# A quarter of the weights' low parts subtracted on GpSimd, and the builder's durations taken from a trace

## The chip, the cores and the metric

The kernel runs on one core of a Trainium2 chip. A core has TensorE (PE; its weight loads are shown as PEld), VectorE (DVE), ScalarE (ACT), GpSimd (POOL) and SyncE (SP), which here issues the loads. The metric is the device time of one execution in microseconds (us). Before the change it is 883.34 us, the median of 3 runs (882.36 to 884.08).

## The reference, cut to what matters

The reference runs four layers over 256 tokens of width 1024, in float32: two attention layers (a sliding window with sinks, then a causal one, phases `a` and `b`), and two layers that each have a mixer of dilated attention and a Mamba-2 scan (`m0`, `m1`) and a SwiGLU feed-forward part of width 2816 (`f0`, `f1`):

```python
def first_block(x, ...):                       # layers a, b
    ...
        q, k, v, z = split_proj(rmsnorm(h, norm_g[i]), w_in_a[j], N_KV_A)
        o = sliding_window_sink_attention(q, k, v, sinks_a[j])
        ...
        o = o.reshape(B, S, MIX_WIDTH) * jax.nn.silu(z)
        h = h + o @ w_out[i]
def second_block(...):                         # layers 0, 1
    ...
        h = h + hybrid_mixer(rmsnorm_2(h, norm_mix[layer]), w_in[layer], ...)
        h = h + swiglu(rmsnorm_2(h, norm_ffn[layer]), w_gate[layer], w_up[layer], w_down[layer])
    return rmsnorm_2(h, final_norm)
```

Most of the arithmetic is `h @ w` with weights that are read once.

## The kernel before

Each weight matrix is cut into units of 256 output columns, and a unit into k-tiles of 128x256. TensorE multiplies in fp32r. To keep float32's precision, each operand is split into a high part (rounded to fp32r) and a low part (the operand less its high part), and a k-tile takes three products: high by high, high by low, low by high. In the phases of the feed-forward part the first two are one matmul of 512 columns (mode `AB`); elsewhere they are separate matmuls of 256 columns.

SyncE loads a weight segment of up to 8 k-tiles (1 MB) into one of three raw buffers (`raw`, `RAW = 3`). `feed` (line 362) then splits two k-tiles at a time: `hi` is a copy on ScalarE, or on VectorE where that is 100 ns less booked, and `lo` is the subtraction `raw - hi` on VectorE (line 396). A raw buffer is free for the next load when both have read it. The 1048 k-tiles of weights make 524 such splits of 128x512 (a few at the start are of one k-tile, and the 16 columns of `dt` are split apart).

Everything else goes beside the weights' matmuls as chains: norms (their power -1/2 runs on GpSimd as a 128x2 tensor_tensor), rotary embedding, attention (scores on TensorE, softmax on VectorE and ScalarE, transposes, values), the convolution and scan of the mixers, gates.

The order on each engine is fixed when the program is built, by a list scheduler. It keeps one planned clock per engine (`self.clk`). `account` (line 251) books every instruction: it starts when its engine's clock and its chain allow, lasts `cost(...)` (line 223), and its result is ready for others `HOP` later. `run_plan` (line 487) emits the next k-tile's matmuls if their inputs are planned to be ready, steps every chain whose inputs are ready on TensorE's planned clock, and lets `feed` split ahead. `feed` waits while VectorE or ScalarE is planned more than `AHEAD` = 500 ns past TensorE, unless fewer than `URGENT` = 5 k-tiles are ready. Fixed pauses in planned time pace attention (`HEAD_A`, `HEAD_B`, `HEAD_0`, `HEAD_1`, `PAIR`), and `calm` (line 269) holds a chain back while VectorE or ScalarE is planned too far ahead. The planned durations thus set the order, not the waits: what waits for what is fixed by the data.

Of the kernel before, what the change touches and what calls it, by code (L numbers as in the profile page):

```python
# [11 lines left out]
F32 = mybir.dt.float32  # L12
F32R = mybir.dt.float32r
BF16 = mybir.dt.bfloat16
# [50 lines left out]
class Engine:  # L65


    def __init__(self, build, name, real):
        self.build, self.ename, self.real = build, name, real
# [43 lines left out]
class Build:  # L113
# [8 lines left out]
    RAW = 3  # L122
    PAGES = 64
    URGENT = 5
    HOP = 100.0
    AHEAD = 500.0
    HEAD_A = 1500.0
    HEAD_B = 1500.0
# [23 lines left out]
    def __init__(self, ctx, tc, io):  # L152
        self.tc = tc
        self.nc = Engines(self, tc.nc)
        self.clk = dict(PE=0.0, DVE=0.0, ACT=0.0, POOL=0.0)
        self.cur = Chain(None, 0.0)
        self.cur.start = 0.0
        self.count = 0
        self.io = io
        self.n = 0  # L160
        self.phase = "i"

        def pool(name, bufs, **kw):
            return ctx.enter_context(tc.tile_pool(name=name, bufs=bufs, **kw))

        self.cp = pool("const", 1)
        self.wraw = pool("wraw", self.RAW)
        self.fp = pool("f", self.PAGES)
        self.xp = pool("x", 4)
        self.up = pool("u", 2)  # L170
        self.hp = pool("h", 6)
        self.sp = pool("s", 8)
        psum = dict(space=bass.MemoryType.PSUM)
        self.pp = pool("psum", 8, **psum)
        self.banks = [0.0] * 8
        self.used = dict(mm=0, sc=0, tr=0, pv=0, out=0)
        self.sides = []
        self.ups = self.raws = 0
        self.planned = {}
        self.landing = 0.0  # L180
        self.live = self.wlive = self.most = 0
        self.kept = {}
        self.x = Timed(self)
        self.res = Timed(self)
        self.plan = []
        self.dma_i = self.cast_i = self.cast_k = self.cast_slot = 0
        self.seg_i = self.seg_k = self.seg_m = self.slot = 0
        self.dma_at = 1200.0
        self.queue = self.nc.sync
        self.units = {}  # L190
        self.bubbles = {}


    def name(self, s):
# [28 lines left out]
    def cost(self, eng, op, args, kw):  # L223
        out = kw.get("out", args[0] if args else None)
        aps = [x for x in list(args) + list(kw.values()) if hasattr(x, "shape")]
        n = 1
        for d in out.shape[1:]:
            n *= d
        cols = sum(1 for x in aps if x is not out and len(x.shape) == 2 and x.shape[1] == 1 and n > 1)
        psum = any("PSUM" in str(getattr(getattr(x, "tensor", x), "space", "")) for x in aps)  # L230
        if eng == "PE":
            if op == "transpose":
                return 110.0
            f32 = args[1].dtype == F32
            if args[1].dtype == BF16:
                return 69.0 if n == 128 else n / 2.4 * 1.02
            if f32 and out.shape[0] == 64:
                return 0.95 * n
            if n < 128:
                return 110.0 * (2 if f32 else 1)  # L240
            return n / 2.4 * (4 if f32 else 1) * 1.02
        if eng == "ACT":
            acc = "accum_out" in kw
            return (52.0 if psum else 93.0) + 0.833 * n + 93.0 * cols
        if eng == "POOL":
            return 650.0
        if op in ("tensor_copy", "tensor_scalar") and not psum:
            return 68.0 + 0.52 * n + 93.0 * cols
        return (130.0 if psum else 68.0) + 1.042 * n + 93.0 * (cols if op != "tensor_tensor_reduce" else 0)

    def account(self, eng, op, args, kw):
        c = self.cur
        dep = max([c.start] + [t for e, t in c.last.items() if e != eng])
        start = max(self.clk[eng], dep)
        end = start + self.cost(eng, op, args, kw)
        self.clk[eng] = end
        self.count += 1
        c.last[eng] = end + self.HOP
        c.ready = max(c.ready, end + self.HOP)


    def go(self, gen):
# [99 lines left out]
    def feed(self):  # L362

        nc = self.nc
        while self.dma_i < len(self.plan) and self.raws < self.RAW:
            self.feed_dma()
        while self.cast_i < self.dma_i and self.cast_slot < self.slot + self.LEAD:
            now = self.clk["PE"]
            urgent = self.cast_slot < self.slot + self.URGENT
            if not urgent and max(self.clk["DVE"], self.clk["ACT"]) > now + self.AHEAD:  # L370
                return
            s = self.plan[self.cast_i]
            if s["at"] > now:
                self.landing = s["at"]
                return
            k = s["k0"] + self.cast_k
            n = min(2, s["k1"] - k)
            if self.wlive >= self.WMIN and self.wlive + self.live + self.SPARE > self.PAGES:
                return
            self.wlive += 2  # L380
            raw = s["raw"][:, self.cast_k:self.cast_k + n, :]
            hi = self.fp.tile([P, n, S], F32R, tag="f", name=self.name("hi"))
            if s["mode"] == "dt":

                both = hi[:, :, 0:32]
                raw, hi, lo = raw[:, :, 0:16], both[:, :, 0:16], both[:, :, 16:32]
            else:
                lo = self.fp.tile([P, n, S], F32R, tag="f", name=self.name("lo"))
            at = s["at"]
            self.cur = Chain(None, at)  # L390
            self.cur.start = at
            if self.clk["DVE"] + self.SWAP < self.clk["ACT"]:
                nc.vector.tensor_copy(hi, raw)
            else:
                nc.scalar.activation(hi, raw, AF.Copy)
            nc.vector.tensor_sub(lo, raw, hi.bitcast(F32))
            for i in range(n):
                s["parts"][k + i] = ((both if s["mode"] == "dt" else hi)[:, i, :], lo[:, i, :], self.cur.ready)
            self.cast_k += n
            self.cast_slot += n  # L400
            if s["k0"] + self.cast_k == s["k1"]:
                self.cast_i += 1
                self.cast_k = 0
                if s["page"]:
                    self.drop()
                else:
                    self.raws -= 1
# [1317 lines left out]
```

## Time and profile before

| | |
|---|---|
| median of 3 runs | 883.34 us (882.36 to 884.08) |
| the profiled execution | 882.25 us, span 880.2 us |
| TensorE busy, mean granted clock | 865.3 us (98%), 0.997 |
| VectorE busy | 731.8 us (83%) |
| ScalarE busy | 556.8 us (63%) |
| GpSimd busy | 14.6 us (2%), 30 instructions |
| read from HBM | 140.15 MB, 160 GB/s over the span |

The span reaches from the first to the last instruction in the profile; the execution's own time holds some 2 us more. Names tell what an instruction writes and reads: `f__lo<-f__raw,f__hi` is a split's subtraction in a feed-forward phase. The prefix is the phase in which the tile was made (`a`, `ao` and so on: an `o` stands for the output projection of the phase). `__p` is a PSUM tile, the other names are SBUF tiles. All of the kernel's instructions carry the line of one helper, L78.

### The profile page before, as it was taken

What the parts mean: (1) busy time and instruction counts of PE and PEld (TensorE: products, weight loads), DVE (VectorE), ACT (ScalarE), POOL (GpSimd) and SP (SyncE); (2) the same over time, 40 slices, a digit from 0 to 9 for tenths busy, and PEclk for the clock granted to TensorE, in tenths of its full rate; (3) what the DMA queues carried; (4) which work ended last, traced back from release to release, by engine and by line L of the source; (5) the groups of instructions that cost most, each with busy time, mean ns of one, the idle gap of its engine ahead of it and who ended that gap; (6) DMA issues with size and microseconds to landing.
All of it is one profiled execution on the core that took longest, in us unless ns stands there. A gap on an engine that the chain in (4) does not pass through costs nothing.

```text
span 880.2 us, 16862 instructions
## 1 busy us (share of the span) xinstructions
PE 865.3 (98%) x6451; PEld 793.9 (90%) x6451; DVE 731.8 (83%) x1652; ACT 556.8 (63%) x1325; POOL 14.6 (2%) x30
## 2 busy tenths in 40 slices
PE   8999999999999999999999999999999999999996
PEld 7987999889999789888888889999899888889996
DVE  6999899998899998899988668889878898998431
ACT  6378763677688885666666445579655666666321
POOL 0000010000000000000000000000000000000000
PEclk9999999999999999999999999999999999999998
DMA  8512673035543046666655637420046665665401
GB/s 315 206 74 73 225 275 130 26 107 177 199 145 108 26 132 215 200 226 224 234 207 179 234 127 274 158 73 25 2 137 217 224 229 200 240 220 187 167 1 48
DMA packets 30385, 142.30 MB, mean 162 GB/s; under 512 B 5344, under 2 KB 6880, under 8 KB 18400
## 3 DMA queue, kind: packets, MB, share of 16 engines
q1 hardware_dynamic: 30016, 141.08, 46.8%
q8 instruction: 51, 0.84, 0.4%
q14 instruction: 30, 0.25, 0.1%
q10 hardware_dynamic: 288, 0.14, 0.1%
HBM read 140.15 MB, written 1.05 MB: 160 GB/s over the span
## 4 chain that ended last, share of the span: by engine, by line
PE 66%; issue 21%; DVE 6%; ACT 4%; DMA 2%; SPq 0%; POOL 0%; POOLq 0%; DVEq 0%
PE m__p L78 20%; PE f__p L78 15%; PE mo__p L78 9%; PE b__p L78 8%; PE fo__p L78 7%; PE bo__p L78 3%; PE ao__p L78 3%; PE a__p L78 1%; DVE a__lo L78 1%; DVE a__sm L78 1%; ACT m__m L78 1%; DMA cst<-cst 1%; DMA fo__raw<-wa 1%; DVE a__pe L78 1%; DVE a__rope L78 1%
## 5 line engine op out<-in xcount | busy, mean ns | idle before, releaser
L78 PE MATMUL f__p<-mo__x,f__hi 128*128 128x512 f32 x492 | 174.6, 396 | 0.0
L78 DVE TENSOR_TENSOR f__lo<-f__raw,f__hi 128x512 fp32r<-128x512 f32 x186 | 123.0, 687 | 21.7 <-ACT f__hi L78 21.1
L78 PE MATMUL f__p<-mo__x,f__lo 128*128 128x256 f32 x492 | 138.0, 280 | 0.0
L78 PEld LDWEIGHTS f__p<-mo__x,f__hi 128*128 128x128 f32 x492 | 92.3, 188 | 21.5
L78 ACT ACTIVATE f__hi<-f__raw 128x512 fp32r<-128x512 f32 x186 | 104.6, 621 | 0.0
L78 PEld LDWEIGHTS f__p<-mo__x,f__lo 128*128 128x128 f32 x492 | 93.0, 189 | 0.0
L78 PE MATMUL fo__p<-f__r,fo__hi 128*128 128x256 f32 (+1 forms) x308 | 74.1, 322 | 0.0
L78 ACT ACTIVATE f__sum<-f__p 128x256 f32<-128x256 f32 x84 | 29.8, 383 | 56.8 <-PE f__p L78 56.7
L78 PE MATMUL f__p<-f__x,f__hi 128*128 128x512 f32 x176 | 63.6, 395 | 0.0
L78 DVE TENSOR_TENSOR m__lo<-m__raw,m__hi 128x512 fp32r<-128x512 f32 x74 | 50.2, 687 | 11.8 <-ACT m__hi L78 11.1
L78 PE MATMUL fo__p<-f__r,fo__lo 128*128 128x256 f32 x208 | 58.5, 281 | 0.0
L78 PEld LDWEIGHTS fo__p<-f__r,fo__hi 128*128 128x128 f32 x308 | 51.4, 190 | 4.4
L78 PE MATMUL m__p<-bo__x,m__hi 128*128 128x256 f32 (+1 forms) x292 | 54.2, 287 | 0.5 <-ACT m__m L78 0.5
L78 PE MATMUL mo__p<-mo__r,mo__hi 128*128 128x256 f32 x288 | 52.5, 284 | 0.0
L78 PE MATMUL a__p<-fo__x,a__hi 128*128 128x256 f32 x272 | 50.8, 287 | 0.7 <-ACT a__hi L78 0.7
L78 PE MATMUL f__p<-f__x,f__lo 128*128 128x256 f32 x176 | 49.3, 280 | 0.0
L78 DVE TENSOR_TENSOR fo__lo<-fo__raw,fo__hi 128x512 fp32r<-128x512 f32 (+1 forms) x60 | 37.3, 669 | 11.9 <-ACT fo__hi L78 9.3
L78 PEld LDWEIGHTS m__p<-bo__x,m__hi 128*128 128x128 f32 (+1 forms) x292 | 44.8, 188 | 2.4 <-issue 1.3
L78 PEld LDWEIGHTS mo__p<-mo__r,mo__hi 128*128 128x128 f32 x288 | 44.8, 192 | 0.2 <-issue 0.2
L78 ACT ACTIVATE m__hi<-m__raw 128x512 fp32r<-128x512 f32 x66 | 40.0, 635 | 7.3 <-DMA m__raw<-w 7.3
L78 PEld LDWEIGHTS a__p<-fo__x,a__hi 128*128 128x128 f32 x272 | 42.1, 191 | 2.1 <-ACT a__hi L78 1.3
L78 ACT ACTIVATE fo__hi<-fo__raw 128x512 fp32r<-128x512 f32 (+2 forms) x61 | 31.7, 580 | 17.4 <-DMA fo__raw<-w 10.0
(540 smaller groups left out, 2465.0 us busy)
## 6 DMA issues: line engine op xcount, KB each, us to landing
f__raw<-wu SPq DMA_DIRECT2D x20, 1024.0 KB, 4.8
f__raw<-wg SPq DMA_DIRECT2D x19, 1024.0 KB, 4.8
m__raw<-w SPq DMA_DIRECT2D x17, 1024.0 KB, 4.8
f__raw<-wd SPq DMA_DIRECT2D x9, 1024.0 KB, 4.9
b__raw<-wb SPq DMA_DIRECT2D x7, 1024.0 KB, 6.4
fo__raw<-wd SPq DMA_DIRECT2D x7, 1024.0 KB, 4.9
mo__raw<-wo SPq DMA_DIRECT2D x12, 512.0 KB, 3.7
fo__raw<-w SPq DMA_DIRECT2D x5, 1024.0 KB, 4.9
```

The lines of the kernel that those rows point to most:

```text
L78: return fn(*args, **kw)
```

## The change

In `feed`, the subtraction goes to GpSimd or to VectorE, whichever the builder plans to finish it sooner; `t` is the time at which the high part is planned to be ready. The split of `dt` stays on VectorE. A counter notes how many went where; about a quarter go to GpSimd. The planned durations and hops are replaced by ones set to those of a trace; GpSimd's was 650 ns for every instruction and is now 950 ns under 64 elements and 100 + 2.3 ns per element above, 1278 ns for a split.

```diff
-    HOP = 100.0
+    HOP = dict(PE=210.0, DVE=140.0, ACT=150.0, POOL=200.0)
...
+        self.share = [0, 0]
...
-            f32 = args[1].dtype == F32
-            if args[1].dtype == BF16:
+            dt, rows = args[1].dtype, args[1].shape[0]
+            if dt == BF16:
                 return 69.0 if n == 128 else n / 2.4 * 1.02
-            if f32 and out.shape[0] == 64:
-                return 0.95 * n
+            if dt == F32R:
+                return max(110.0, 6.7 + 0.4427 * n)
             if n < 128:
-                return 110.0 * (2 if f32 else 1)
-            return n / 2.4 * (4 if f32 else 1) * 1.02
+                return 224.0
+            if out.shape[0] == 64:
+                return 15.0 + 1.0 * n
+            if rows == 64:
+                return 44.0 + 0.92 * n
+            return 1.69 * n
         if eng == "ACT":
-            acc = "accum_out" in kw
-            return (52.0 if psum else 93.0) + 0.833 * n + 93.0 * cols
+            acc = kw.get("accum_out") is not None
+            return (52.0 if psum else 93.0) + 0.833 * n + 93.0 * (cols - acc) + 93.0 * acc
         if eng == "POOL":
-            return 650.0
+            return 950.0 if n < 64 else 100.0 + 2.3 * n
+        if op == "reciprocal":
+            return 195.0
+        if op == "tensor_copy" and out.dtype == F32R:
+            return 68.0 + 0.754 * n
         if op in ("tensor_copy", "tensor_scalar") and not psum:
-            return 68.0 + 0.52 * n + 93.0 * cols
-        return (130.0 if psum else 68.0) + 1.042 * n + 93.0 * (cols if op != "tensor_tensor_reduce" else 0)
+            return 68.0 + 0.52 * n + 63.0 * cols
+        if op == "stream_shuffle":
+            return 100.0 + 1.042 * n
+        return 78.0 + 1.042 * n + 63.0 * (cols if op != "tensor_tensor_reduce" else 0)
...
-        c.last[eng] = end + self.HOP
-        c.ready = max(c.ready, end + self.HOP)
+        c.last[eng] = end + self.HOP[eng]
+        c.ready = max(c.ready, end + self.HOP[eng])
...
-            nc.vector.tensor_sub(lo, raw, hi.bitcast(F32))
+
+            t = max(t for t in self.cur.last.values())
+            late = [max(t, self.clk[e]) + self.cost(e, "tensor_sub", (lo, raw), {}) for e in ("DVE", "POOL")]
+            sub = nc.gpsimd if late[1] <= late[0] and s["mode"] != "dt" else nc.vector
+            sub.tensor_sub(lo, raw, hi.bitcast(F32))
+            self.share[sub is nc.gpsimd] += 1
```

## Rows read from the trace of the kernel before

**Rows 1.** The page's first part: busy us (share of the span) and instructions per engine.

```profile
PE 865.3 (98%) x6451; PEld 793.9 (90%) x6451; DVE 731.8 (83%) x1652; ACT 556.8 (63%) x1325; POOL 14.6 (2%) x30
```

**Rows 2.** Waits of TensorE: who waited for whom, us in total, times, longest.

```profile
PE a__p L78 <- ACT fo__x L78: 1.1, 1, 1.1
...
PE m__p L78 <- ACT m__m L78: 0.7, 2, 0.5
...
PE ao__p L78 <- DVE a__s L78: 0.6, 1, 0.6
PE mo__p L78 <- ACT mo__pt L78: 0.6, 1, 0.6
PE ao__p L78 <- DVE ao__r L78: 0.4, 1, 0.4
PE mo__p L78 <- ACT mo__xg L78: 0.4, 1, 0.4
```

**Rows 3.** Busy time by stretch: stretch and length, each engine's busy us (xinstructions), clock, DMA.

```profile
40.00:80.00 40.00, 39.41 (x332) 33.40 (x331) 38.99 (x139) 29.76 (x100) 0.00 (x0) 1.00 0.23 80
240.00:320.00 80.00, 78.69 (x681) 72.18 (x680) 76.23 (x192) 67.55 (x192) 0.31 (x3) 1.00 0.29 93
340.00:540.00 200.00, 200.00 (x1199) 178.18 (x1198) 166.43 (x320) 121.16 (x257) 0.69 (x1) 1.00 0.61 211
680.00:820.00 140.00, 140.00 (x837) 123.42 (x836) 123.12 (x224) 88.82 (x182) 1.07 (x1) 1.00 0.64 220
820.00:860.00 40.00, 40.00 (x337) 40.00 (x337) 15.00 (x24) 12.54 (x24) 0.00 (x0) 1.00 0.14 48
```

**Rows 4.** Groups of VectorE over the span: xcount | busy us, mean ns | idle before.

```profile
L78 DVE TENSOR_TENSOR f__lo<-f__raw,f__hi 128x512 fp32r<-128x512 f32 x186 | 123.0, 687 | 21.7 <-ACT f__hi L78 21.1
L78 DVE TENSOR_TENSOR m__lo<-m__raw,m__hi 128x512 fp32r<-128x512 f32 x74 | 50.2, 687 | 11.8 <-ACT m__hi L78 11.1
```

**Rows 5.** Groups of VectorE between 40 and 80 us.

```profile
L78 DVE TENSOR_TENSOR a__lo<-a__raw,a__hi 128x512 fp32r<-128x512 f32 x16 | 10.8, 687 | 0.1
...
L78 DVE TENSOR_TENSOR a__rope<-a__rope,a__rot 128x512 f32<-128x512 f32 x4 | 2.7, 687 | 0.0
```

**Rows 6.** Groups of VectorE between 240 and 320 us.

```profile
L78 DVE TENSOR_TENSOR m__lo<-m__raw,m__hi 128x512 fp32r<-128x512 f32 x33 | 22.7, 687 | 3.3 <-ACT m__hi L78 3.0
L78 DVE TENSOR_TENSOR m__acc<-m__acc,m__tap 128x512 f32<-128x512 f32 x14 | 9.6, 685 | 0.0
L78 DVE TENSOR_TENSOR m__m<-m__m,m__cb 128x512 f32<-128x512 f32 x12 | 8.1, 684 | 0.0
```

**Rows 7.** Four powers of GpSimd in order of time: start us, us, what.

```profile
115.90 2.79 POOL L78 TENSOR_TENSOR b__s<-b__s,mhalf 128x2 f32<-128x2 f32 x1 [91.00 <-ACT b__hi L78]
...
223.55 0.69 POOL L78 TENSOR_TENSOR m__s<-m__s,mhalf 128x2 f32<-128x2 f32 x1 [1.30 <-PE m__p L78]
...
365.33 0.69 POOL L78 TENSOR_TENSOR f__s<-f__s,mhalf 128x2 f32<-128x2 f32 x1 [30.73 <-DVE f__s L78]
...
637.09 1.06 POOL L78 TENSOR_TENSOR m__s<-m__s,mhalf 128x2 f32<-128x2 f32 x1 [36.72 <-DVE m__s L78]
```

**Rows 8.** VectorE in order of time, beside those powers.

```profile
115.64 2.49 DVE L78 TENSOR_TENSOR b__lo<-b__raw,b__hi 128x512 fp32r<-128x512 f32 x4
...
365.17 0.75 DVE L78 TENSOR_TENSOR f__sum<-f__p,f__sum 128x256 f32<-128x256 f32 x2
...
636.93 0.68 DVE L78 TENSOR_TENSOR m__lo<-m__raw,m__hi 128x512 fp32r<-128x512 f32 x1
637.53 0.69 DVE L78 TENSOR_TENSOR m__acc<-m__acc,m__tap 128x512 f32<-128x512 f32 x1
638.16 0.69 DVE L78 TENSOR_TENSOR m__lo<-m__raw,m__hi 128x512 fp32r<-128x512 f32 x1
```

**Rows 9.** Low parts' tiles (f__lo; m__lo from 310.5 us): xcount, durations, first and last start.

```profile
L78 DVE TENSOR_TENSOR f__lo<-f__raw,f__hi x186: 680/685/694, 366.4 to 804.8; 128x512 fp32r<-128x512 f32 x186
...
L78 PE MATMUL fo__p<-f__r,f__lo x112: 279/282/286, 478.2 to 828.9; 128*128 128x256 f32 x112
...
L78 PE MATMUL mo__p<-m__r,m__lo x10: 279/283/288, 310.6 to 314.2; 128*128 128x256 f32 x10
L78 DVE TENSOR_TENSOR m__lo<-m__raw,m__hi x2: 683/684/685, 311.1 to 313.0; 128x512 fp32r<-128x512 f32 x2
```

## The prediction

> **What bounds the kernel now.** I read the shares of the engines first. TensorE is busy for 865.3 of 880.2 us, VectorE for 731.8, ScalarE for 556.8, and GpSimd for 14.6 [rows 1]. TensorE bounds the kernel, if its busy time is full. A matmul's modelled end overlaps the next one, so "busy" does not prove that. I therefore compared the pace of stretches in the table of busy time by stretch: from 820 to 860 us VectorE works for only 15.0 of 40 us, nothing holds TensorE up, and it runs 337 matmuls; from 40 to 80 us, with VectorE at 38.99 of 40 us, it runs 332, some of them the dearer fp32 ones of attention [rows 3]. So even where VectorE is full, TensorE keeps nearly its free pace.
>
> Next I read TensorE's waits. They are eleven rows of 7.8 us in all, from 1.1 down to 0.4 us each. Five, of 2.7 us together, lie between the start and the tail: the softmax sums (0.6) and the split of the gated output (0.4) from VectorE, the decay factors (0.7), the transposed probabilities (0.6) and the scaled inputs of the scan (0.4) from ScalarE [rows 2]. That is about what a relieved VectorE and better planning can give back: 0.3% of the span.
>
> Last I asked where VectorE has room. Between 40 and 80 us it idles 40.00 - 38.99 = 1.0 us, between 240 and 320 us 80.00 - 76.23 = 3.8 us. In the two FFN stretches it idles 200 - 166.4 = 33.6 and 140 - 123.1 = 16.9 us [rows 3].
>
> **The change part by part.** The weights are 1048 k-tiles, and one split takes two: 524 subtractions of 128x512, each 0.687 us long on VectorE [rows 4]. Issued back to back they cost it less: four take 2.49 us, so 0.60 us follows from (2.49 - 0.69) / 3 [rows 8]. A quarter is 131, so VectorE loses 131 x 0.60 = 79 us of work. Where TensorE is full that is worth nothing. It is worth something only at the two waits that VectorE ends: -1.0 us. The three waits on ScalarE stay.
>
> The price on GpSimd is not in this trace. Its nearest rows are the power of a 128x2 tile, 0.69 us, and the longest of them, 2.79 us [rows 7]; the edit itself writes 100 + 2.3 x 512 = 1278 ns. I take 1.28 us, which lies between these rows; 131 of them are 168 us, a fifth of the span, so GpSimd has room.
>
> What they do to VectorE decides. The small power shows it. It takes 0.69 us at 223.55 us, when VectorE is idle, and 0.69 us at 365.33 us, when VectorE adds from PSUM. It takes 1.06 us at 637.09 us: VectorE had just begun a subtraction with two SBUF inputs at 636.93, which ended at 637.61, and the power ended 0.54 us behind that. It takes 2.79 us at 115.90 us, beside four such subtractions in a row, which end at 118.13 us; it ends 0.56 us later [rows 7, 8]. So GpSimd stands still while VectorE reads two tensors from SBUF. The reverse shows only faintly, since the power reads two elements: the next VectorE instruction after 637.53 starts 0.63 us later instead of 0.60 [rows 8]. A GpSimd subtraction that reads 2 x 512 elements can hold VectorE between 0 and its whole 1.28 us. Nearly all that fills VectorE in these stretches has two SBUF inputs (splits, conv taps, decay products, rotary sums [rows 4 to 6]), and the builder picks GpSimd only where VectorE's planned clock is 667 ns or more behind the ready time, so VectorE has work waiting. I take 1.0 us.
>
> By that, one move takes 0.60 us from VectorE and gives it 1.0 us of standing still: +0.4 us, over 131 moves +52 us. The FFN stretches have room for their part (50 us idle), and there the low parts lie ready for long: the last split of the second FFN's up and gate tiles starts at 804.8 us, and matmuls read such tiles until 828.9 us [rows 9]. The tight stretches have none. They hold 16 + 33 = 49 splits [rows 5, 6]. Since a VectorE backlog is what the builder looks for, I put 40% of them, 20, on GpSimd rather than a quarter: 20 x 0.4 = 8 us more VectorE time against 4.8 us idle, +3 us. The ends of the range: at no hold, -20 x 0.60 = -12 us of VectorE time, which is worth at most the 2.7 us of waits; at the full 1.28 us hold, 20 x 0.68 = 14 us against 4.8, +9 us.
>
> The Trainium skill, SBUF — State Buffer, section "Who interferes with whom", says that a VectorE instruction with two SBUF inputs contends with a GpSimd instruction that reads SBUF, and that the one that starts later blocks fully. The power's four times bear out GpSimd's half of it; no row shows a long GpSimd instruction. By the rule in full the hold is the whole instruction, and the case with +9 us is the one to come.
>
> The new durations and hops change the order in which the builder emits. They add and remove no instruction. Before, the builder took a 256-column matmul for 109 ns; it now takes 120 ns, and costs VectorE less for PSUM sources (78 instead of 130 ns ahead of the elements), so its plan sees less backlog and advances attention earlier against the weight slots. Its plan had slack against the chip, and that slack goes: a chain step planned to be just in time is late by any hold. Four attention stages (a, b, m0, m1) each end where TensorE waits for such a chain; I charge one hold of 1.0 us each, +4 us. Its bounds are -1.7 us (the other three waits go too, through longer hops) and about 4 x 2.79 = +11 us (each stage loses what the longest power lost).
>
> Queues: on GpSimd's own queue the powers of the norms and the memsets of the conv inputs now stand behind subtractions. Each can be 1.28 us later. The scale rows that wait for the powers are used by units whose matmuls have already run, and other units' matmuls cover that; I take 0, at most one 1.28 us per norm, and the last one at 873 us has no split near it. A raw buffer is freed up to 0.6 us later, so SyncE issues the next load later; three buffers and a load per eight k-tiles leave room, 0. A matmul that now waits for GpSimd holds all matmuls behind it on TensorE.
>
> Sum: the profiled execution took 882.25 us (its span of 880.2 and 2.05 around it). 882.25 - 1 + 3 + 4 = 888.3 us, +6. The median of the three runs, 883.34, is 1.1 us above that execution, so I predict 889 us.
>
> **The rivals.**
> 1. Faster: GpSimd runs beside VectorE without holding it. For it: VectorE lost only 0.03 us at 637.53 [rows 8]. Against it: the waiting power. It gives back the five mid-span waits, 2.7 us: 880.6 us. It decides once the hold is under the 0.60 us that a move saves.
> 2. No change: the holds fall into the FFN stretches and the leads there swallow them; or fewer splits move in the tight stretches than I think, since the better durations show the builder less backlog. For it: TensorE's pace hardly differs between stretches [rows 3]. 883 us.
> 3. Slower by much: GpSimd is the one that starves. VectorE runs its instructions back to back, and the low part comes late by the 2.1 us that the power lost (2.79 - 0.69) on top of 1.28 us. Around 311 to 314 us a low part has no such lead: a split starts at 313.0 and ends by 313.7, and matmuls on such tiles start until 314.2 us [rows 9]. If 8 of the 20 moves stall TensorE for 2.1 us, that is +17 us: 900 us.
>
> **How the numbers follow.** Forecast (slower, some 885 to 897): 0.38. Rival 3: 0.12. Rival 2: 0.23. Rival 1: 0.27. The two slower cases make 0.50. Less than 0.2%, 1.8 us, is what a measurement of this kernel can't tell from no change. The range runs from 879.5 (the waits gone, and a little from the order) to 905 (rival 3 with the full hold), and leaves out less than 2 in 10.
>
> **What would show it.** Right: VectorE instructions longer than 0.687 us, or starting late beside a GpSimd subtraction; VectorE's busy time growing where it was full; GpSimd's subtractions well above 1.28 us where VectorE is full; TensorE's waits on low parts and on attention's chains growing from 2.7 us to 8 or more. Wrong: GpSimd subtractions of 1.28 us beside unchanged VectorE spacing of 0.60 us, and TensorE's waits at 2.7 us or below. The sign is wrong if the attention stretches run fewer TensorE waits than now.

## The result, and the profile after

The changed kernel takes 945.98 us, the median of 4 runs (944.07 to 949.01), against 883.06 us (882.36 to 884.08) for the kernel before beside it: ratio 1.0715, 95% interval 1.0694 to 1.0737. It is 63 us slower; the prediction said 889 us, with 905 as the upper end. The profiled execution took 949.01 us, its span 946.7 us.

The page of the changed kernel, engine totals and granted clock in 40 slices (tenths of full speed):

```profile
PE 890.3 (94%) x6451; PEld 812.8 (86%) x6451; DVE 782.3 (83%) x1558; ACT 532.7 (56%) x1265; POOL 202.8 (21%) x163
...
PEclk9999989799899999989999999999999899999998
```

Against [rows 1], VectorE lost 94 instructions and gained 50.5 us of busy time. GpSimd has 133 instructions more, the moved subtractions. TensorE runs the same 6451 matmuls, yet is busy 25.0 us longer, and its other time grew from 880.2 - 865.3 = 14.9 to 946.7 - 890.3 = 56.4 us. So the 66.5 us of span are 41.5 us in which TensorE stands and 25.0 us in which it works more slowly.

The waits of TensorE in the changed kernel (who waited for whom, us in total, times, longest):

```profile
PE b__p L78 <- DVE b__rope L78: 9.7, 1, 9.7
PE f__p L78 <- DVE f__sm L78: 9.4, 2, 5.0
PE m__p L78 <- DVE m__sm L78: 4.0, 2, 3.8
PE fo__p L78 <- ACT fo__hg L78: 3.5, 1, 3.5
PE b__p L78 <- DVE b__sm L78: 3.4, 1, 3.4
...
PE m__p L78 <- POOL m__s L78: 0.4, 1, 0.4
```

Where [rows 2] had no row above 1.1 us, five are now 3.4 us and more: a rotary embedding, the sums of norms (the three rows of `sm`, which TensorE multiplies by `ones`) and, in the tail, the scaled output `hg`. They are steps of chains, all but the last on VectorE. None of the twenty rows names a low part, from either engine. GpSimd appears with one power, 0.4 us.

Busy time by stretch in the changed kernel (columns as in [rows 3]), first 40 to 860 us in parts, then the longest stall and two stretches of half clock:

```profile
40.00:360.00 320.00, 296.29 (x2417) 272.63 (x2415) 286.36 (x700) 208.53 (x545) 64.67 (x50) 0.96 0.35 122
360.00:420.00 60.00, 52.28 (x351) 48.15 (x352) 49.69 (x73) 32.83 (x65) 19.64 (x14) 0.94 0.61 211
420.00:580.00 160.00, 160.00 (x907) 138.82 (x907) 132.29 (x219) 79.82 (x179) 38.07 (x27) 1.00 0.50 172
580.00:720.00 140.00, 137.42 (x1143) 127.81 (x1141) 124.34 (x269) 92.47 (x230) 24.56 (x24) 0.99 0.37 127
720.00:760.00 40.00, 33.96 (x212) 30.64 (x211) 33.20 (x52) 25.04 (x50) 13.50 (x11) 0.91 0.66 239
760.00:860.00 100.00, 100.00 (x578) 88.15 (x578) 86.35 (x130) 45.70 (x101) 23.38 (x18) 1.00 0.45 156
...
160.00:165.00 5.00, 5.00 (x44) 5.00 (x43) 4.79 (x11) 2.44 (x3) 1.29 (x1) 1.00 0.35 129
165.00:175.00 10.00, 0.32 (x3) 0.12 (x1) 9.76 (x17) 3.95 (x8) 4.38 (x3) 0.77 0.11 39
175.00:178.00 3.00, 2.94 (x14) 2.29 (x15) 3.00 (x11) 0.88 (x1) 0.00 (x0) 0.50 0.86 311
...
402.50:409.40 6.90, 5.92 (x20) 5.19 (x21) 5.33 (x11) 1.29 (x3) 1.67 (x1) 0.51 0.72 259
...
sum 42.60, PE 40.52 PEld 37.52 DVE 29.74 ACT 11.54 POOL 8.71; mean PE 5.07 PEld 4.69 DVE 3.72 ACT 1.44 POOL 1.09
```

The bodies of the two FFN parts (420 to 580 and 760 to 860 us) run with TensorE full, at full clock, as in [rows 3], although they hold some 45 of the moved subtractions. The loss lies outside them: 23.7 us of standing in 40 to 360 us (2.8 in the same stretch before), 7.7 in 360 to 420 us, 6.0 in 720 to 760 us. From 165 to 175 us TensorE runs three matmuls while VectorE is busy 9.76 of 10 us; from 175 us the granted clock is 0.50, the lower of its two levels (1.2 GHz). The last line is the sum over all eight stretches at that level: 40.52 us of TensorE's work. Three matmuls of 256 columns take 0.64 us there and 0.36 us at full clock, so I estimate that some 18 of the 40.52 us are lost to the clock: most of the 25.0.

The order of time on VectorE, then GpSimd, in that stall (start us, us, what):

```profile
168.08 0.68 DVE L78 TENSOR_TENSOR b__rope<-b__p,b__tq 128x512 f32<-128x512 f32 x1
168.67 1.33 DVE L78 TENSOR_SCALAR t<-t,cst 128x256 f32<-128x256 f32 x1
170.04 0.43 DVE L78 TENSOR_SCALAR t<-t 128x512 f32<-128x512 f32 x1
170.38 1.76 DVE L78 TENSOR_TENSOR b__rot<-b__rot,b__tq 128x512 f32<-128x512 f32 x1
172.06 2.35 DVE L78 TENSOR_TENSOR b__lo<-b__raw,b__hi 128x512 fp32r<-128x512 f32 x2
174.33 0.68 DVE L78 TENSOR_TENSOR b__rope<-b__rope,b__rot 128x512 f32<-128x512 f32 x1
...
168.58 1.27 POOL L78 TENSOR_TENSOR b__lo<-b__raw,b__hi 128x512 fp32r<-128x512 f32 x1 [5.49 <-ACT b__hi L78]
170.14 3.11 POOL L78 TENSOR_TENSOR b__lo<-b__raw,b__hi 128x512 fp32r<-128x512 f32 x2 [0.29 <-ACT b__hi L78]
```

GpSimd begins a subtraction at 168.58 and ends it at 169.85 us. VectorE's 128x256 operation, begun at 168.67, ends at 170.00 us: 1.33 us, where the twice as large one behind it takes 0.43 and the same operation in the kernel before 0.35:

```profile
159.58 0.35 DVE L78 TENSOR_SCALAR t<-t,cst 128x256 f32<-128x256 f32 x1
```

Beside GpSimd's next two, the rotary product takes 1.76 us (0.69 in the trace before) and two subtractions 2.35 instead of 0.69 + 0.60 us [rows 8]. At 168.08, fed from PSUM, an operation takes 0.68 us. The final `b__rope`, for which TensorE waits, ends at 175.01 us. The holds make some 3 us of the 9.7 (0.98 + 1.07 + 1.06); VectorE spends the rest on this chain's own steps and on work that it had queued ahead of them, such as angles for the rotary tables of later phases.

Groups of VectorE, then GpSimd, in the changed kernel (xcount | busy us, mean ns | idle before):

```profile
L78 DVE TENSOR_TENSOR f__lo<-f__raw,f__hi 128x512 fp32r<-128x512 f32 x110 | 91.3, 861 | 3.6 <-ACT f__hi L78 1.1
L78 DVE TENSOR_TENSOR f__sum<-f__p,f__sum 128x256 f32<-128x256 f32 x84 | 31.6, 415 | 1.1 <-ACT f__sum L78 1.0
L78 DVE TENSOR_TENSOR f__sum<-f__sum,f__rowh 128x512 f32<-128x512 f32 x22 | 30.2, 1374 | 0.6
L78 DVE CAST f__hi<-f__raw 128x512 fp32r<-128x512 f32 x18 | 7.6, 422 | 0.0
...
L78 POOL TENSOR_TENSOR f__lo<-f__raw,f__hi 128x512 fp32r<-128x512 f32 x46 | 61.3, 1336 | 180.5 <-ACT f__hi L78 130.1 <-DVE f__sum L78 39.5 <-PE f__p L78 10.9
L78 POOL TENSOR_TENSOR b__lo<-b__raw,b__hi 128x512 fp32r<-128x512 f32 x15 | 22.9, 1536 | 23.6 <-ACT b__hi L78 23.6
```

Two of these groups in the kernel before:

```profile
L78 DVE TENSOR_TENSOR f__sum<-f__p,f__sum 128x256 f32<-128x256 f32 x84 | 31.5, 417 | 1.0 <-ACT f__sum L78 1.0
L78 DVE TENSOR_TENSOR f__sum<-f__sum,f__rowh 128x512 f32<-128x512 f32 x22 | 15.1, 685 | 0.0
```

VectorE's subtractions rose from 687 ns in [rows 4] to 861 ns, and a product of two SBUF tensors from 685 ns before to 1374 ns, while the addition from PSUM stayed at 415 ns (417 before), although 36 of the 84 lie beside a GpSimd subtraction. With every VectorE instruction held against the median of its like in the trace before, 117 are over 100 ns longer, by 1.02 us in the median and 1.12 at most: 109 us in all, 0.82 us for each moved subtraction. The Trainium skill, SBUF — State Buffer, section "Who interferes with whom", says that the pair of SBUF ports that VectorE shares with GpSimd is an exclusive lock, whose loser blocks fully. That agrees with 1.02 of 1.27 us, less what the held instruction came late.

### The profile page after: what moved, and what is told of

Read it like the earlier page. It is cut to its first block, busy times and chain, and to the rows that moved or that the text cites. A ratio compares the mean times of both kernels' runs of the same rounds, so it can differ in the third digit from the quotient of the medians.

```text
span 946.7 us, 17141 instructions
## 1 busy us (share of the span) xinstructions
PE 890.3 (94%) x6451; PEld 812.8 (86%) x6451; DVE 782.3 (83%) x1558; ACT 532.7 (56%) x1265; POOL 202.8 (21%) x163
## 4 chain that ended last, share of the span: by engine, by line
PE 52%; DVE 25%; issue 8%; DMA 8%; ACT 6%; POOL 0%; DVEq 0%; SPq 0%; POOLq 0%; ACTq 0%
PE f__p L78 25%; PE m__p L78 12%; PE fo__p L78 7%; PE b__p L78 4%; PE mo__p L78 3%; DVE m__lo L78 2%; DMA fo__raw<-wd 1%; DVE m__xs L78 1%; DMA ao__raw<-wb 1%; DVE a__lo L78 1%; DVE a__sm L78 1%; DVE m__acc L78 1%; DVE b__lo L78 1%; DMA b__raw<-wo 1%; DVE m__t L78 1%
## 5 line engine op out<-in xcount | busy, mean ns | idle before, releaser
L78 PE MATMUL f__p<-f__x,f__hi 128*128 128x512 f32 x292 | 103.9, 395 | 0.0
L78 PE MATMUL f__p<-mo__x,f__hi 128*128 128x512 f32 x288 | 102.4, 395 | 0.0
L78 POOL TENSOR_TENSOR f__lo<-f__raw,f__hi 128x512 fp32r<-128x512 f32 x46 | 61.3, 1336 | 180.5 <-ACT f__hi L78 130.1
L78 PE MATMUL f__p<-f__x,f__lo 128*128 128x256 f32 x292 | 81.9, 280 | 0.0
L78 PE MATMUL f__p<-mo__x,f__lo 128*128 128x256 f32 x288 | 80.8, 280 | 0.0
L78 PEld LDWEIGHTS f__p<-f__x,f__hi 128*128 128x128 f32 x292 | 54.7, 187 | 12.8
L78 PEld LDWEIGHTS f__p<-mo__x,f__hi 128*128 128x128 f32 x288 | 54.0, 187 | 12.6
L78 PE MATMUL fo__p<-f__r,fo__lo 128*128 128x256 f32 x200 | 56.4, 282 | 0.0
L78 PEld LDWEIGHTS f__p<-f__x,f__lo 128*128 128x128 f32 x292 | 55.2, 189 | 0.0
L78 PEld LDWEIGHTS f__p<-mo__x,f__lo 128*128 128x128 f32 x288 | 54.4, 189 | 0.0
L78 PE MATMUL fo__p<-f__r,f__hi 128*128 128x256 f32 (+1 forms) x180 | 44.5, 330 | 0.0
```

Of the source, the lines that this page charges most:

```text
L78: return fn(*args, **kw)
```

## The experiments

Each was timed beside the kernel before (882.1 to 882.3 us in these comparisons). VectorE, TensorE: busy us of the profiled execution. Moved: low parts made by GpSimd. Held: the lengthening of VectorE's instructions, counted as above, in us.

| run | median us | ratio, 95% interval | VectorE | TensorE | moved | held |
|---|---|---|---|---|---|---|
| e1_costs_only | 885.84 | 1.0044 (1.0027 to 1.0061) | 743.3 | 865.4 | 0 | - |
| e2_split_old_costs | 927.38 | 1.0505 (1.0489 to 1.0521) | 772.1 | 885.5 | 132 | 103 |
| e3_after_order_on_vector | 910.13 | 1.0311 (1.0295 to 1.0326) | 753.7 | 875.5 | 0 | - |
| e4_before_order_on_gpsimd | 885.46 | 1.0031 (1.0019 to 1.0043) | 740.9 | 867.8 | 131 | 89 |
| e5_book_hold | 951.24 | 1.0790 (1.0757 to 1.0823) | 779.8 | 885.9 | 235 | 184 |
| e6_book_half | 942.75 | 1.0678 (1.0655 to 1.0702) | 782.4 | 890.5 | 158 | 130 |
| e7_unbooked_quarter | 895.47 | 1.0146 (1.0129 to 1.0163) | 745.6 | 872.8 | 0 | - |
| e8_lead20 | 934.31 | 1.0583 (1.0558 to 1.0609) | 787.7 | 882.6 | 136 | 114 |
| e9_new_order_every_fourth | 902.35 | 1.0235 (1.0213 to 1.0258) | 758.0 | 875.3 | 131 | 95 |
| e10_before_order_chosen | 930.07 | 1.0541 (1.0525 to 1.0557) | 776.5 | 880.6 | 245 | 191 |
| e11_before_order_chosen_half | 898.72 | 1.0182 (1.0165 to 1.0199) | 758.5 | 873.7 | 141 | 113 |
| e12_after_order_no_read | 883.86 | 1.0019 (1.0007 to 1.0032) | 681.6 | 867.9 | 133 (zeros) | 2 |

**Which half of the change.** The new durations alone, every subtraction on VectorE:

```diff
-            sub = nc.gpsimd if late[1] <= late[0] and s["mode"] != "dt" else nc.vector
-            sub.tensor_sub(lo, raw, hi.bitcast(F32))
+            nc.vector.tensor_sub(lo, raw, hi.bitcast(F32))
```

> The new durations and hops alone; every subtraction stays on VectorE. Theory A (the hold: a GpSimd subtraction stops VectorE for some 0.8 to 1.0 us): near before, 878 to 892 us, TensorE idle under 20 us, no VectorE subtraction longer than 0.70 us. Theory B (the order made from the new durations lets splits run ahead of the chains): most of the 63 us stay, 925 to 950 us, with low parts ready 15 us or more before their matmuls.

Measured +3.5 us, in theory A's range, with 15.6 us in which TensorE does nothing. The choice of engine with the old durations (only GpSimd's is the new one, 100 + 2.3 ns per element):

```diff
-    HOP = dict(PE=210.0, DVE=140.0, ACT=150.0, POOL=200.0)
+    HOP = 100.0
...
-            return 950.0 if n < 64 else 100.0 + 2.3 * n
+            return 650.0 if n < 64 else 100.0 + 2.3 * n
```

> The choice of engine alone, with the durations and hops of before (GpSimd booked with 1278 ns for a split). Theory A: slow like the changed kernel, 915 to 950 us. Theory B: near before, 880 to 895 us, although as many splits or more go to GpSimd.

Measured +45 us, again in theory A's range. The choice makes most of the loss, under the old durations too.

**The order or the hold.** The changed kernel's order, with the moved subtractions run on VectorE in their place:

```diff
+            if sub is nc.gpsimd:
+                self.account("POOL", "tensor_sub", (lo, raw, hi.bitcast(F32)), {})
+                self.tc.nc.vector.tensor_sub(lo, raw, hi.bitcast(F32))
```

> The changed kernel's order on every engine, but the 133 subtractions chosen for GpSimd run on VectorE, in the place where they were emitted. VectorE gets 133 x 0.60 = 80 us back and loses the holds, 109 us by the changed kernel's trace. Theory A: 885 to 905 us. Theory B: as slow as the changed kernel or slower, 935 to 965 us, since the order is what stalls TensorE.

Measured +28 us, between the two and nearer to theory A. From here to the changed kernel the plan is the same and 133 subtractions change their engine: another 36 us, though VectorE loses that work. The counterpart: the order of before, every fourth subtraction run on GpSimd, but booked on VectorE.

```diff
+            if s["mode"] != "dt" and self.cast_slot // 2 % 4 == 3:
+                self.account("DVE", "tensor_sub", (lo, raw, hi.bitcast(F32)), {})
+                self.tc.nc.gpsimd.tensor_sub(lo, raw, hi.bitcast(F32))
```

> The order of before on every engine, but every fourth split's subtraction (131) runs on GpSimd. Theory A: each holds VectorE for 0.8 us and saves 0.60 us, so that attention's chains come late: 905 to 945 us. Theory B: 883 to 893 us, since the leads of the order of before take it up.

Measured +3 us, in theory B's range; theory A missed by 20 us. The holds are there (89 us), but VectorE's busy time grows by only 9.1 us, since the moves relieve it by nearly as much. So the number of moved splits does not decide by itself.

**Does the plan lack the hold?** That gave a theory: the order of before had spare time for VectorE, and the changed plan spends it on a relief that doesn't come. So the hold was booked on VectorE's planned clock, whole (820 ns) and by half (410 ns):

```diff
             self.share[sub is nc.gpsimd] += 1
+            if sub is nc.gpsimd:
+                self.clk["DVE"] = max(self.clk["DVE"], t) + 820.0
```

> The changed kernel, but the builder also books 820 ns on VectorE for each subtraction that goes to GpSimd (109 us / 133, the mean hold in the changed kernel's trace). VectorE then looks later, and 235 subtractions go to GpSimd instead of 133. Theory C (the loss comes from VectorE time that the plan leaves out, 109 us in the changed kernel, 80 us in the one with its order on VectorE: splits fill VectorE's planned idle time, so chain steps queue behind them): nothing is left out, so 884 to 905 us although more is moved. Theory D (the choice moves subtractions at the worst moments, where VectorE is full): worse than the changed kernel, 950 to 1010 us.

> As the run that books 820 ns, with 410 ns; 158 subtractions go to GpSimd, and some 65 us of VectorE stay out of the plan. Theory C: between the two, 900 to 925 us. Theory D: 945 to 970 us.

Measured +69 and +61 us: both miss theory C. The first lies in theory D's range, the second 2 us below it. A later planned clock makes the rule pick GpSimd more often (235 and 158 splits), which adds holds; VectorE's busy time stays at 780 to 782 us. With no holds at all, a quarter booked on GpSimd but run on VectorE, under the old durations:

```diff
+            if s["mode"] != "dt" and self.cast_slot // 2 % 4 == 3:
+                self.account("POOL", "tensor_sub", (lo, raw, hi.bitcast(F32)), {})
+                self.tc.nc.vector.tensor_sub(lo, raw, hi.bitcast(F32))
```

> The durations and hops of before, nothing on GpSimd, but every fourth split's subtraction is booked on GpSimd in the plan while it runs on VectorE: 131 x 0.60 = 79 us left out of the plan, evenly, with no hold. Theory C: 900 to 920 us, like the 910 us of the changed order on VectorE. Theory D: 882 to 890 us, since the moved ones aren't chosen by backlog.

Measured +13 us, between the two ranges: a plan that relies on work which is not taken away from VectorE does cost, but a fifth of the 63 us. The last of this set limits how far splits run ahead:

```diff
-    LEAD = 60
+    LEAD = 20
```

> The changed kernel with splits allowed only 20 k-tiles ahead of the matmuls (LEAD) instead of 60. Theory C: fewer splits stand in front of chain steps, 890 to 925 us. Theory D: no help, 940 to 960 us.

Measured 934.31 us, 12 us better than the changed kernel with more VectorE time (787.7 us), again between the two ranges: letting splits run far ahead makes a part of the loss, and the smaller one.

**Which splits are moved.** The order of the new durations (as in e1), every fourth on GpSimd:

```diff
+            if s["mode"] != "dt" and self.cast_slot // 2 % 4 == 3:
+                self.account("DVE", "tensor_sub", (lo, raw, hi.bitcast(F32)), {})
+                self.tc.nc.gpsimd.tensor_sub(lo, raw, hi.bitcast(F32))
```

> The order that the new durations make with every subtraction booked on VectorE (the run with the new durations alone, 886 us), but every fourth split's subtraction runs on GpSimd (131). If the order of before had spare time on VectorE that the order of the accurate durations lacks: 900 to 925 us. If the places of the moved subtractions decide: 886 to 894 us, like every fourth one in the order of before (885 us).

Measured +20 us, in the first range, where the order of before took the same treatment for +3. Next the order of before with the splits that the rule picks, every one (below) and, with a counter, every second:

```diff
+            t = max(t for t in self.cur.last.values())
+            pool = max(t, self.pool_at) + 1278.0
+            if pool <= max(t, self.clk["DVE"]) + 611.0 and s["mode"] != "dt":
+                self.pool_at = pool
+                self.account("DVE", "tensor_sub", (lo, raw, hi.bitcast(F32)), {})
+                self.tc.nc.gpsimd.tensor_sub(lo, raw, hi.bitcast(F32))
```

> As the run with every other one, with all 245 that the rule picks. If the places decide: 925 to 960 us, near the 951 us of the run that booked the hold and moved 235. If what the plan leaves out decides: 890 to 910 us, as VectorE's net load grows by some 245 x (0.8 - 0.6) = 50 us.

> The order of before on every engine; 141 subtractions run on GpSimd, every other one of those that the rule of the changed kernel picks (where VectorE's planned clock is late), still booked on VectorE. If the places decide: holds of 1.0 us where VectorE is full, 900 to 930 us against the 885 us of every fourth. If the time that the plan leaves out decides: 884 to 892 us.

Measured +48 and +16 us. The first is where the places were said to put it, the second just under that range and above the other. Against e4 the second one moves only ten splits more in the same order, but a moved split holds VectorE for 0.80 us instead of 0.68: the rule picks those during which VectorE has work waiting.

**The hold taken away.** The order of the changed kernel once more. GpSimd writes zeros into the tiles of its 133 low parts and reads nothing, so a quarter of the low products is lost:

```diff
+            if sub is nc.gpsimd:
+                self.account("POOL", "tensor_sub", (lo, raw, hi.bitcast(F32)), {})
+                self.tc.nc.gpsimd.memset(lo.bitcast(F32), 0.0)
```

> The changed kernel's order on every engine, but in place of the 133 subtractions GpSimd writes zeros into those low parts (this leaves out a quarter of the low parts): VectorE is relieved as the plan believes, and GpSimd reads nothing from SBUF. If the hold makes the loss: no long VectorE subtractions, 880 to 892 us. If the new order itself is bad wherever the subtractions run: 905 us or more.

Measured 883.86 us, +1.6 us. The page of this run, its largest waits of TensorE, and a VectorE and a GpSimd group, each from its own view:

```profile
PE 867.9 (98%) x6451; PEld 795.4 (90%) x6451; DVE 681.6 (77%) x1558; ACT 538.7 (61%) x1265; POOL 81.1 (9%) x163
```

```profile
PE i__p L543 <- DVE warm L540: 1.1, 1, 1.1
PE a__p L78 <- ACT fo__x L78: 1.0, 1, 1.0
PE b__p L78 <- DVE b__sm L78: 0.9, 1, 0.9
```

```profile
L78 DVE TENSOR_TENSOR f__lo<-f__raw,f__hi 128x512 fp32r<-128x512 f32 x110 | 72.2, 686 | 4.0 <-ACT f__hi L78 1.4
...
L413 POOL MEMSET f__lo<- 128x512 f32 x56 | 29.7, 535 | 219.7 <-DVE f__gt L78 75.7 <-DVE f__sum L78 68.2 <-PE f__p L78 46.5
```

The order is the same as in the changed kernel, and so is the count of instructions of each engine. VectorE's subtractions are back at 686 ns, its busy time is 100.7 us less, the longest wait is 1.1 us, and the mean granted clock is 0.997 instead of 0.972. The zeros take 0.53 instead of 1.3 us and need no high part, but TensorE did not wait for GpSimd's low parts in the changed kernel either. So without the reads of GpSimd, and the holds they cause, the loss of 945.98 - 883.86 = 62 us is gone. That is so in this order: e3 shows that 80 us of subtractions without any hold cost 28 us in it. What counts is VectorE's time, spent on work or on holds. One rival goes with the reads too: a raw buffer that GpSimd reads late is filled again late. But in e10 ScalarE waits for loads for 59 us in all, as in the kernel before (58 us), and 48 us are lost.

The Trainium skill, SBUF — State Buffer, section "Who interferes with whom", says that VectorE's two-input instruction contends with a GpSimd instruction that reads SBUF, not with one that only writes it; the 686 ns agree.

**The time against VectorE's load.** Within one order, the runs change only which subtractions VectorE does and which hold it. Order of before: +9.1 us of VectorE time cost +3 us (e4), +26.7 cost +16 (e11), +44.7 cost +48 (e10). Order of after: -50.2 cost +2 (e12), +21.9 cost +28 (e3), +50.5 cost +63. In each order more load costs more, but the order counts as well: +21.9 in that of after cost 28, +26.7 in that of before 16. In the order of before some 10 us vanish in idle time, and beyond that each further us costs 0.75 (e4 to e11) to 1.7 us (e11 to e10), although VectorE idles for 148 us before. Between 40 and 340 us of the kernel before it idles only 24.3 us (this row; the next is e10 in the same stretch, the third e4):

```profile
40.00:340.00 300.00, 297.20 (x2508) 274.27 (x2507) 275.66 (x737) 214.29 (x572) 6.79 (x11) 1.00 0.40 133
```

```profile
40.00:340.00 300.00, 288.06 (x2399) 262.95 (x2398) 275.76 (x640) 207.26 (x558) 112.95 (x84) 0.99 0.37 122
```

```profile
40.00:340.00 300.00, 296.29 (x2493) 273.19 (x2492) 277.38 (x697) 213.57 (x570) 63.97 (x49) 1.00 0.39 131
```

VectorE is busy for the same 276 to 277 us in all three: the holds hardly went into its idle time, they pushed other work back. In e10 TensorE has run 109 matmuls fewer by then, in e4 15. No version beat the kernel before, and e12, with 50 us of VectorE's work simply gone, was not faster: TensorE's time without work is 881.9 - 867.9 = 14.0 us there, and was 14.9.

## Why the prediction was wrong

- **What bounds the kernel: right.** A relief of VectorE was said to be worth about 1 us; in e12 TensorE's time without work falls by 0.9 us, and the kernel is not faster.
- **The hold: right in kind, and near in size.** Taken 1.0 us for each moved split, measured 1.02 (median) for each of the 117 instructions that were held, 0.82 over all 133 moves. GpSimd's subtraction was taken at 1.28 us and takes 1.27 undisturbed, 1.29 to 1.62 in the means of its groups.
- **VectorE's total: right by luck, as two errors cancel.** Forecast +52 us, measured +50.5. But the holds less the relief are only 109 - 80 = +29 us. The other 22 us are work that either engine can do, sent from ScalarE to VectorE by a plan that thinks VectorE relieved: e3, without any hold, has VectorE at 753.7 us, +21.9, and ScalarE at 537.8, -19.0. The 18 copies of `f__hi` on VectorE in the rows of after are some of it; no such group stood there before (all copies of high parts on VectorE went from 22 to 42). "They add and remove no instruction" was wrong: by the new durations alone (e1) VectorE has 25 instructions more and ScalarE 36 fewer.
- **The step that failed: "20 x 0.4 = 8 us more VectorE time against 4.8 us idle, +3 us".** It took the 120 us of two sampled stretches for all the tight ones. The FFN bodies swallow their moves, as forecast, but they hold only 45 of the 133 (27 and 18); 58 lie before 420 us, 25 between 580 and 760 us and 6 behind 860 us (one is counted on both sides of a bound). At these 88 VectorE has little room. At the forecast's own 0.4 us that is 35 us, not 8. Measured is 41.5 us more of standing TensorE. The 40% that the forecast moved in the tight stretches was too much: 58 of the 223 subtractions before 420 us moved, 26%, and 25 to 28% in the stretches from there to 860 us. What was too small was the part of the span that counts as tight.
- **The term left out: TensorE's clock.** The sum had none for it. Behind the stalls TensorE works 40.5 us at half its clock (none of it in the kernel before ahead of the tail), and its busy time grows by 25.0 us.
- **The new durations: +4 charged, +3.5 measured alone (e1), by luck.** The +4 were four holds at the ends of chains, and e1 has no hold. With the choice the durations cost more: 63 us, and 45 with the old ones (e2).
- **GpSimd's queue: 0 charged.** In the waits of TensorE one power stands for 0.4 us.
- **The rivals.** "GpSimd runs beside VectorE without holding it" fell with 117 held instructions. "No change" assumed that the holds fall into the FFN stretches; a third of the moves did. "GpSimd starves" gave 900 us by late low parts, and TensorE waits for none. The forecast looked for the price at a few chain ends and the third rival at the low parts; it is VectorE's load over all the stretches outside the FFN bodies.
- **Open.** How much of the 62 us would stay if the clock did not fall was not tried, nor which share comes from splits that stand ahead of chain steps; e8's 12 us is the only measure of it. Why the order of the new durations takes the same moves for +20 instead of +3 us is explained only by the 11.5 us of VectorE time that it has more to begin with (e1).

## What to carry to other kernels

Before work goes from VectorE to GpSimd, subtract: what a move saves (0.60 us here) less how long it holds VectorE's two-input work (0.68 us for splits taken at even distance, 0.82 for those picked where VectorE has a backlog). Then ask in which stretches the moved work lies, count all of them and not a sample, and take an engine's idle time there rather than its share over the span. Where TensorE is full, add the clock it loses behind each new stall.

## What the runs showed of the hardware beyond that

A GpSimd instruction that only writes SBUF held no subtraction of VectorE (686 ns in e12), one that reads two tensors held VectorE's instructions by 1.02 us. Not only two-tensor operations are held: the 128x256 `TENSOR_SCALAR` at 168.67 us, with one large SBUF input, took 1.33 instead of 0.35 us. Some operations with one input were held even by a GpSimd instruction that only writes: in e12 seven `TENSOR_SCALAR` beside the zeros took 0.14 to 0.40 us longer, 2.2 us in all. One of them is the second of this pair, with the zeros beside it:

```profile
147.16 1.01 DVE L78 TENSOR_SCALAR b__kk<-b__kk 128x256 f32<-128x256 f32 x2
...
147.50 0.53 POOL L413 MEMSET b__lo<- 128x512 f32 x1 [0.72 <-ACT t L78]
```

In the kernel before such a pair takes 0.62 us. Additions fed from PSUM were not held (415 ns beside 417).
